# Experts' rows added to the stream in DRAM by scatters, instead of being gathered at the end

## The chip, the cores and the metric

The kernel runs on one core of a Trainium2 chip. The time is that of the device, in microseconds (us), the median of several executions. The core has a tensor engine (PE), three other compute engines (DVE, ACT, POOL), a queue processor that issues DMAs (SP), and 16 DMA engines that all queues share.

## The reference

One layer of a hybrid decoder for 512 tokens of 1024 values, all in float32. What matters here is its last part, the experts:

```python
h  = h + concat(rmsnorm_A(oA), rmsnorm_B(oB)) @ w_out      # attention, two groups of heads
h  = h + cross-attention(rmsnorm(h) -> rmsnorm(mem))
h  = h + hierarchical MoE(rmsnorm(h))   # top-1 group of 4, then top-2 of its 4 SwiGLU experts
out = rmsnorm_final(h)
```

There are 16 experts in 4 groups. Each has a gate and an up matrix (1024 x 256) and a down matrix (256 x 1024): 3.15 MB of weights. A token goes to two experts of one group, and their results come back to it with a weight each.

## The kernel before

The first three quarters of the span are the projections, the attentions and the router. The residual stream of the 512 tokens is held in SBUF as `HO`, four tiles (t = 0 to 3) of 128 tokens by 1024 values. The router writes the normed tokens to a DRAM tensor `T`, and for each expert a list of its tokens (up to 128 places, `lists`; with more, a path that this input doesn't take).

Then 16 experts follow one another (e = 0 to 15). For each:

- SP loads the weights in six units of 512 KB (four of gate and up, in two DMAs of 256 KB each, and two of down, one DMA each; line L736) into a ring of buffers, far ahead.
- POOL gathers the expert's rows of `T` into `xe` with an indirect DMA (L1130), four experts ahead.
- ACT casts each unit into a high part `wh` (L708) and DVE makes the low part `wl` (L709); PE multiplies with three products of parts for one product (L136 to L138).
- PE's sums for gate and up go through a sigmoid on ACT (`sg`, L1216) and DVE, are transposed, and ACT casts them into `hh` (L1229). Then PE does the down projection (`dn`).
- ACT scales the result by the tokens' weights into `y` (128 places by 1024, L1263; three buffers), and SP writes `y` to the expert's rows of a DRAM tensor `Y` (L1264). A row of zeros stands at the end of `Y`.

This holds for experts 0 to 13. The last two (`LATE = NE - 2`) don't go through DRAM: their rows stay in SBUF in two parts (L1252, L1253), DVE makes one-hot matrices `P` of their tokens' places (L1213), and PE spreads their rows over the tokens by products with `P` (`combine`, L1193), 32 matmuls in all. While expert 14 runs, POOL begins eight indirect gathers with accumulation `HO<-Y,slot` (L1269): for each tile of tokens and each of a token's two choices they fetch the row of `Y` with the number in `slot` and add it to `HO` in SBUF. A choice that is a late expert fetches the zero row. The two gathers of one tile must follow one another.

At the end POOL loads the gain of the last norm (L1279), DVE adds PE's sums to `HO` (L1288), ACT sums the squares (L1289), DVE multiplies by the norm and the gain (L1296), and SP writes the output (L1298).

The order of the instructions on each engine is set by a scheduler from the order of the code and from the tiles' buffers; an engine, and a DMA queue, takes its instructions in that order.

Of the kernel before, what the change touches and what calls it, by code (L numbers as in the profile page):

```python
# [11 lines left out]
F32 = mybir.dt.float32  # L12
# [9 lines left out]
S = 512  # L22
D = 1024
# [11 lines left out]
LATE = NE - 2  # L35
# [3 lines left out]
def layer(ctx, tc, a, out, dbg=None):  # L39
# [24 lines left out]
    # ---------------------------------------------------------------- helpers  # L64
    # a weight unit is 1024 values a partition: loaded whole, then split into two float32r parts
    W = {}

    # the places of a weight's tiles, in turn: (pool, tag count) for the raw unit and for its parts
# [71 lines left out]
    # -------------------------------------------------------------- constants  # L140
# [17 lines left out]
    # ================================================= phase 1: projection, FoX, SB  # L158
# [43 lines left out]
    # ---- forget gates  # L202
# [20 lines left out]
    # ---- pieces  # L223
# [82 lines left out]
    # what the heads give, by feature: the heads of a pair share a tile  # L306
# [3 lines left out]
    # the tokens come last first: the keys of a query block are its own block and those behind it;  # L310
    # the products of a pair's heads run side by side in the columns of the tensor engine
# [15 lines left out]
    # blocks of queries that are handled together  # L327
# [16 lines left out]
    # the features of a pair of heads go to their place; their squares are summed over the pairs  # L344
# [141 lines left out]
    # ================================================= memory keys and values  # L486
# [45 lines left out]
    # ================================================= phase 2: out projection, cross attention  # L532
# [16 lines left out]
    # the products of each run of a weight's rows are finished on their own  # L549
# [95 lines left out]
    # two heads of two tiles of tokens  # L645
# [47 lines left out]
    # ================================================= router  # L693
# [5 lines left out]
    # half a unit split: the parts take turns in halves of tiles  # L699
# [42 lines left out]
    Y = dram.tile([LATE * CAP + 1, D], F32, name="Y")  # L742
    # the token and the weight of every place in the experts' lists; rows of their own for what has none
    L = dram.tile([NE * CAP + 2 * S, 2], I32, name="L")
    zero8 = rt.tile([128, 8], F32, name="zero8")
    nc.gpsimd.memset(zero8, 0.0)
    nc.gpsimd.dma_start(Y[LATE * CAP:, :].rearrange("o (p c) -> (o p) c", p=128), zero8)
    zeroi = rt.tile([128, NE, 2], I32, name="zeroi")
    nc.gpsimd.memset(zeroi, 0)
    nc.gpsimd.dma_start(L[0:NE * CAP, :].rearrange("(p e) c -> p e c", e=NE), zeroi)  # L750
    # the gain of the norm goes into the router's weights, so that the router reads HO itself
# [30 lines left out]
    # of two equal logits the first wins: (i, 0, j) is one for j < i, (i, 1, j) for j > i  # L782
# [10 lines left out]
    # what a place holds, by token and choice: the token, then the bits of the weight  # L793
    put = rp.tile([128, 2, NT, 2], I32, name="put")
    nowhere = rtile([2, NT], "nowhere")
    for n in range(2):
        nc.gpsimd.iota(put[:, n, :, 0], pattern=[[128, NT]], base=0, channel_multiplier=1)
# [22 lines left out]
    # one half of a token tile of HO through the router's product  # L820
# [20 lines left out]
    def route(t):  # L841
# [8 lines left out]
        # the rank of a logit among the four of its set: the groups, or the experts of a group  # L850
# [14 lines left out]
        # places of the tile's tokens in the lists of their experts, plus one  # L865
# [9 lines left out]
        # the first expert's tokens come from HO itself: a one-hot of their places times the norm  # L875
# [41 lines left out]
    # the last experts' rows are spread by the tensor engine: their tokens (plus one) by place  # L917
    lidx = rp.tile([128, NE - LATE], F32, name="lidx")
    lists = rp.tile([128, NE, 2], I32, name="held")
    idx = rp.tile([128, FIRST], I32, name="idx")  # L920
    cnti = rp.tile([128, NE + 1], I32, name="cnti")
    slots, places = [], []
# [31 lines left out]
    # the place of a token's choice in the list of its expert, and its expert  # L954
# [35 lines left out]
    def slot_numbers(step):  # L990
        for n, (pv, ev, ok) in [(step, places[step])] if step < 2 else ():
            in_y = rtile([NT], f"iny{n}")
            nc.vector.scalar_tensor_tensor(in_y, ev, float(LATE), ok, op0=OP.is_lt, op1=OP.mult)
            sf = rtile([NT], f"sf{n}")
            nc.vector.scalar_tensor_tensor(sf, ev, float(CAP), pv, op0=OP.mult, op1=OP.add)
            nc.vector.scalar_tensor_tensor(sf, sf, float(-LATE * CAP), in_y, op0=OP.add, op1=OP.mult)
            nc.vector.tensor_scalar(sf, sf, float(LATE * CAP), None, op0=OP.add)
            si = rp.tile([128, NT], I32, name=f"slot{n}")
            nc.vector.tensor_copy(si, sf)
            slots.append(si)  # L1000
        if step < 2:
            return
        cmax = rp.tile([128, 1], F32, name="cmax")
        nc.vector.reduce_max(cmax, cnt, axis=AX.X)
        nc.vector.tensor_copy(cnti[:, 0:NE], cnt)
        nc.vector.tensor_copy(cnti[:, NE:NE + 1], cmax)
# [15 lines left out]
    # ================================================= experts with more than CAP tokens  # L1022
# [101 lines left out]
    # ================================================= experts  # L1124
# [65 lines left out]
    # the rows of a late expert, spread over a tile of tokens  # L1190
# [5 lines left out]
    for e in range(NE):  # L1196
# [9 lines left out]
        if e in (4, 6, 8):  # L1206
            with tc.issue_after(W["hid"].ins):
                slot_numbers(e // 2 - 2)
# [10 lines left out]
        if e == NE - 1:  # L1219
            spread = [dnp.tile([128, 512], F32, name="dn") for _ in range(2)]  # L1220
            for nh in range(2):
                combine(spread[nh], 0, nh, 0)
# [33 lines left out]
        # the weights of the first experts come late  # L1256
        if not late:
            waiting.append((e, y, dps))
        if e not in range(1):
            for n, y, dps in waiting:  # L1260
                with tc.issue_after(W["last"].ins):
                    for nh in range(2):
                        nc.scalar.activation(y[:, nh * 512:nh * 512 + 512], dps[nh], AF.Copy, scale=wof(n))  # L1263
                nc.sync.dma_start(Y[n * CAP:(n + 1) * CAP, :], y)  # L1264
            waiting.clear()
        if e == LATE:
            for n in range(2):
                for t in range(NT):
                    nc.gpsimd.indirect_dma_start(  # L1269
                        out=HO[:, t, :], out_offset=None, in_=Y[:, :],  # L1270
                        in_offset=bass.IndirectOffsetOnAxis(ap=slots[n][:, t:t + 1], axis=0),
                        compute_op=OP.add)
# [3 lines left out]
    # ================================================= combine, final norm  # L1276
    mark("combine")
    g_fin = etile([D])
    nc.gpsimd.dma_start(g_fin, a["norm_final"].partition_broadcast(128))  # L1279
    junk = etile([2, 512], F32)  # L1280
    for t in range(NT):
        ss = small.tile([128, 2], F32, name="ssf")
        for nh in range(2):
            cs = slice(nh * 512, nh * 512 + 512)
            cp = spread[nh] if t == 0 else dnp.tile([128, 512], F32, name="dn")
            for n in range(1 if t == 0 else 0, NE - LATE):
                combine(cp, t, nh, n)
# [39 lines left out]
```

## Time and profile before

| | us |
|---|---|
| median of 3 runs (664.9 to 665.46) | 665.44 |
| span of the profiled execution | 662.1 |
| PE busy in it | 625.6 (94%) |
| DVE, ACT, POOL busy | 461.6, 376.7, 53.1 |
| share of the chain that ended last: PE, DMA | 82%, 6% |

The profiled execution has no time of its own beside its span; the three runs' times are 665.46, 665.44 and 664.9 us. The span goes from the first to the last instruction of the core. A DMA isn't an instruction of an engine that computes: its issue is short, and its landing comes later. The DMA share is the mean busy share of the 16 DMA engines; the fullest windows of this profile show a little over 1.

### The profile page before, as it was taken

To read this page: it belongs to the slowest core of one execution; us is meant where nothing else is said; L and a number is where in the kernel's file an instruction comes from. 1 tells how busy PE (TensorE), PEld (TensorE's weight loads), DVE (VectorE), ACT (ScalarE), POOL (GpSimd) and SP (SyncE) were. 2 spreads that over 40 slices of the span, in tenths; PEclk is the share of its full clock that TensorE was granted. 3 is DMA by queue.
4 is the path that set the end of the run, shared out by engine and by line. 5 is a ranking of instruction groups with operands and counts; after the bars stand their busy time and mean duration, and the time that the engine had idled before them with its cause. 6 is when DMAs were issued, how large, how long until landed. Compare 5 with 4: busy or idle time off the path is not lost.

```text
span 662.1 us, 10336 instructions
## 1 busy us (share of the span) xinstructions
PE 625.6 (94%) x3595; PEld 507.4 (77%) x3596; DVE 461.6 (70%) x941; ACT 376.7 (57%) x752; POOL 53.1 (8%) x80
## 2 busy tenths in 40 slices
PE   3999999999999999999999999999999999999980
PEld 2988777888877888988888898867767777777750
DVE  4843794963497797855853466347879999989955
ACT  5632556653456676613632354333369898898842
POOL 2000000000000000000000003000152011010350
PEclk9999999999999999999999999999999999999996
DMA  8545744323764634561453223792989999999494
GB/s 279 171 125 133 186 113 116 92 65 92 171 157 107 169 104 152 200 218 35 121 166 96 77 84 88 260 367 99 313 258 366 378 388 380 386 383 385 130 201 174
DMA packets 105497, 128.91 MB, mean 195 GB/s; under 512 B 8456, under 2 KB 82240, under 8 KB 105440
## 3 DMA queue, kind: packets, MB, share of 16 engines
q1 hardware_dynamic: 101120, 114.43, 54.8%
q0 software_dynamic: 4320, 13.77, 7.6%
q8 instruction: 29, 0.48, 0.3%
q14 instruction: 28, 0.23, 0.1%
HBM read 103.96 MB, written 11.56 MB: 174 GB/s over the span
## 4 chain that ended last, share of the span: by engine, by line
PE 82%; DMA 6%; DVE 4%; ACT 3%; issue 2%; POOL 1%; SPq 1%; DVEq 0%; POOLq 0%
PE pj L136 8%; PE pj L138 8%; PE pj L137 8%; PE o L315 5%; PE gu L136 4%; PE pja L136 4%; PE gu L137 4%; PE gu L138 4%; PE pja L137 4%; PE pja L138 4%; PE tr L322 3%; PE tr L129 3%; PE pjb L137 3%; PE pjb L136 3%; PE pjb L138 3%; PE dn L136 2%
## 5 line engine op out<-in xcount | busy, mean ns | idle before, releaser
L90 DVE TENSOR_TENSOR wl<-w,wh 128x1024 fp32r<-128x1024 f32 (+1 forms) x64 | 78.3, 1223 | 81.3 <-ACT wh L89 75.1
L89 ACT CAST wh<-w 128x1024 fp32r<-128x1024 f32 (+1 forms) x64 | 67.2, 1050 | 104.5 <-PE pj L137 37.3
L709 DVE TENSOR_TENSOR wl<-w,wh 128x512 fp32r<-128x512 f32 x168 | 108.5, 686 | 5.5 <-ACT wh L708 5.1
L708 ACT CAST wh<-w 128x512 fp32r<-128x512 f32 x168 | 96.6, 621 | 12.8 <-PE gu L138 9.8
L136 PE MATMUL pj<-uh,wh 128*128 128x512 f32 x128 | 52.1, 407 | 0.0
L138 PE MATMUL pj<-uh,wl 128*128 128x512 f32 x128 | 51.5, 403 | 0.0
L137 PE MATMUL pj<-ul,wh 128*128 128x512 f32 x128 | 51.2, 400 | 0.0
L136 PE MATMUL gu<-wh,xh 128*128 128x512 f32 x120 | 48.5, 404 | 0.2 <-ACT xh L131 0.2
L138 PE MATMUL gu<-wh,xl 128*128 128x512 f32 x120 | 47.6, 397 | 0.0
L137 PE MATMUL gu<-wl,xh 128*128 128x512 f32 x120 | 47.1, 393 | 0.0
L136 PE MATMUL pj<-wh,uh 128*128 128x256 f32 (+1 forms) x128 | 37.7, 294 | 2.3 <-ACT uh L131 2.3
L138 PE MATMUL pj<-wh,ul 128*128 128x256 f32 (+1 forms) x128 | 37.5, 293 | 0.0
L137 PE MATMUL pj<-wl,uh 128*128 128x256 f32 (+1 forms) x128 | 37.3, 292 | 0.0
L315 PE MATMUL o<-pT,V 128*64 128x128 f32 x320 | 33.0, 284 | 0.1
L136 PE MATMUL pja<-wh,fmh 128*128 128x512 f32 x80 | 32.4, 405 | 0.0
L137 PE MATMUL pja<-wl,fmh 128*128 128x512 f32 x80 | 31.9, 399 | 0.0
L138 PE MATMUL pja<-wh,fml 128*128 128x512 f32 x80 | 31.8, 398 | 0.0
L315 PEld LDWEIGHTS o<-pT,V 128*64 128x64 f32 x320 | 21.4, 136 | 10.0 <-issue 5.2
L136 PEld LDWEIGHTS pj<-uh,wh 128*128 128x128 f32 x128 | 24.1, 188 | 6.3 <-issue 1.7
L138 PEld LDWEIGHTS pj<-uh,wl 128*128 128x128 f32 x128 | 24.1, 188 | 5.9 <-issue 0.9
L368 ACT ACTIVATE p<-lg,nm 128x512 f32<-128x512 f32 (+3 forms) x32 | 16.9, 527 | 20.4 <-DVE nm L366 20.3
L137 PEld LDWEIGHTS pj<-ul,wh 128*128 128x128 f32 x128 | 24.1, 188 | 4.8 <-issue 0.3
(356 smaller groups left out, 1633.2 us busy)
## 6 DMA issues: line engine op xcount, KB each, us to landing
w<-in_w_exp_gate_dram SPq DMA_DIRECT2D x64, 256.0 KB, 7.6
w<-in_w_exp_up_dram SPq DMA_DIRECT2D x64, 256.0 KB, 7.6
w<-in_w_exp_down_dram SPq DMA_DIRECT2D x32, 512.0 KB, 7.6
w<-in_w_in_dram SPq DMA_DIRECT2D x24, 512.0 KB, 4.1
w<-in_w_xkv_dram SPq DMA_DIRECT2D x16, 512.0 KB, 4.4
Y<-y SPq DMA_DIRECT2D x14, 512.0 KB, 8.7
KH<-th SPq DMA_DIRECT2D x32, 128.0 KB, 2.3
w<-in_w_out_dram SPq DMA_DIRECT2D x8, 512.0 KB, 4.3
```

Of the source, the lines that this page charges most:

```text
L89: nc.scalar.copy(h, raw)
L90: nc.vector.tensor_sub(l, raw, h)
L129: nc.tensor.transpose(pt[:, j, :], src[:, k * 128:(k + 1) * 128], ident)
L136: nc.tensor.matmul(o, lh, rh, start=start, stop=False)
L137: nc.tensor.matmul(o, lh, rl, start=False, stop=False)
L138: nc.tensor.matmul(o, ll, rh, start=False, stop=stop)
L315: nc.tensor.matmul(o[hh * HD:(hh + 1) * HD, i * 128:(i + 1) * 128], V[:, s, vcol + hh * HD:vcol + (hh + 1) * HD], pTs[hh][:, at + s - i, : ...
L322: nc.tensor.transpose(pt[:, s, :], p[:, s * 128:(s + 1) * 128], ident)
L368: nc.scalar.activation(p_[:, cs], lg[:, cs], AF.Exp, bias=nm, scale=1.0, accum_out=sm)
L708: nc.scalar.copy(h, raw)
L709: nc.vector.tensor_sub(l, raw, h)
```

## The change

A DRAM tensor `H2` (512 rows and 128 spare ones) gets the stream `HO` when the router has read it, by four writes on SP's queue. `y` of experts 0 to 14 is not written to a place of its own but added to its tokens' rows of `H2`, by an indirect DMA with accumulation on POOL's queue (a scatter, one for each expert); the lists get a third column with the row to add to, and empty places add to the spare rows. When the last scatter has landed, SP loads the four tiles of `HO` back from `H2`, and the gain of the last norm too. Only expert 15 is spread by one-hot products (`LATE = NE - 1`): 16 matmuls, none of them ahead of its own down projection. `Y`, its zero row, the numbers `slot` and the eight gathers are gone.

```diff
-LATE = NE - 2
+LATE = NE - 1
...
-    Y = dram.tile([LATE * CAP + 1, D], F32, name="Y")
+    H2 = dram.tile([S + CAP, D], F32, name="H2")
-    L = dram.tile([NE * CAP + 2 * S, 2], I32, name="L")
+    L = dram.tile([NE * CAP + 2 * S, 3], I32, name="L")
...
         nc.sync.dma_start(T[t * 128:(t + 1) * 128, :], u)
+        nc.sync.dma_start(H2[t * 128:(t + 1) * 128, :], HO[:, t, :])
...
-        if e in (4, 6, 8):
+        if e == 8:
             with tc.issue_after(W["hid"].ins):
-                slot_numbers(e // 2 - 2)
+                counts()
...
-        if e == NE - 1:
-            spread = [dnp.tile([128, 512], F32, name="dn") for _ in range(2)]
-            for nh in range(2):
-                combine(spread[nh], 0, nh, 0)
...
-                nc.sync.dma_start(Y[n * CAP:(n + 1) * CAP, :], y)
+                nc.gpsimd.indirect_dma_start(
+                    out=H2[:, :], out_offset=bass.IndirectOffsetOnAxis(ap=lists[:, n, 2:3], axis=0),
+                    in_=y, in_offset=None, compute_op=OP.add)
             waiting.clear()
         if e == LATE:
-            for n in range(2):
-                for t in range(NT):
-                    nc.gpsimd.indirect_dma_start(
-                        out=HO[:, t, :], out_offset=None, in_=Y[:, :],
-                        in_offset=bass.IndirectOffsetOnAxis(ap=slots[n][:, t:t + 1], axis=0),
-                        compute_op=OP.add)
+            g_fin = etile([D])
+            nc.sync.dma_start(g_fin, a["norm_final"].partition_broadcast(128))
+            for t in range(NT):
+                nc.sync.dma_start(HO[:, t, :], H2[t * 128:(t + 1) * 128, :])
...
-    g_fin = etile([D])
-    nc.gpsimd.dma_start(g_fin, a["norm_final"].partition_broadcast(128))
```

POOL's instructions in the experts' stage, before: the gathers of the experts' rows stand one behind another, and behind them the eight accumulating gathers of the end and the gain.

```order
L1130 DMA xe<-T,idx 128x1024
L1130 DMA xe<-T,held 128x1024 x12
L1269 DMA HO<-Y,slot_5675 128x1024 x4
L1269 DMA HO<-Y,slot_5905 128x1024 x4
L1279 DMA w<-in_norm_final_dram 128x1024
L1029 TENSOR_LOAD cnti
```

POOL's instructions now, in the middle of the stage (`y_5802`, `y_5913` and `y_6024` are the rows of experts 5, 6 and 7, `xe_5852` is expert 9's, and each scatter also waits for the scatter before it to land):

```order
L1120 DMA xe_5852<-T_4375,held_5085 128x1024
L1250 DMA H2_4376<-y_5802,held_5085 640x1024
L1120 DMA xe_5963<-T_4375,held_5085 128x1024
L1250 DMA H2_4376<-y_5913,held_5085 640x1024
L1250 DMA H2_4376<-y_6024,held_5085 640x1024
L1120 DMA xe_6074<-T_4375,held_5085 128x1024
L1120 DMA xe_6189<-T_4375,held_5085 128x1024
L1250 DMA H2_4376<-y_6139,held_5085 640x1024
```

Between the gathers now stand the scatters, one for each expert to 14, so that a gather can have a scatter ahead of it that waits; the gathers of the end are gone.

SP's end of the stage, before: the last weight loads (the two of the down matrix are expert 15's), then the writes of experts 12 and 13, then the output.

```order
L736 DMA w<-in_w_exp_gate_dram 128x2x256
L736 DMA w<-in_w_exp_up_dram 128x2x256
L736 DMA w<-in_w_exp_down_dram 128x1024 x2
L1029 TENSOR_LOAD cnti
L1029 ISA x2
L1264 DMA Y<-y 128x1024 x2
L1298 DMA out_dram<-w 128x512 x8
```

The same end of SP's queue now:

```order
L736 DMA w_6720<-in_w_exp_down_dram 128x1024
L736 DMA w_6722<-in_w_exp_down_dram 128x1024
L1019 TENSOR_LOAD cnti_5087
L1019 ISA x2
L1258 DMA HO_81<-H2_4376 128x1024 x3
L1256 DMA w_6899<-in_norm_final_dram 128x1024
L1258 DMA HO_81<-H2_4376 128x1024
L1282 DMA out_0_dram<-w_6929 128x512 x2
```

The writes of `y` have left SP's queue, where they stood behind the weights, and the four loads of `HO` and the gain stand ahead of the output.

ACT's instructions while expert 14 ends, now (they stand the same way before, with `w_6732` and L1229; `w_6720` is the first down unit of expert 15, `hh_6789` and `y_6801` are expert 14's):

```order
L708 CAST wh_5259<-w_6711 128x512
L1206 ACTIVATE sg_6783<-gu_6742 128x256
L708 CAST wh_5259<-w_6714 128x512
L708 CAST wh_5261<-w_6720 128x512
L1215 CAST hh_6789<-tr_6786 128x256
L708 CAST wh_5262<-w_6720 128x512
L708 CAST wh_5260<-w_6714 128x512
L1249 ACTIVATE y_6801<-dn_6802,held_5085 128x512
```

Nothing moved here: in both kernels a cast of expert 15's down unit stands ahead of expert 14's `hh`.

## Rows read from the trace of the kernel before

**Rows 1.** The page: the span
```profile
span 662.1 us, 10336 instructions
```

**Rows 2.** Timeline of DVE at the end: start, length (us), line, operation
```profile
650.93 0.68 DVE L1288 TENSOR_TENSOR HO<-dn,HO 128x512 f32<-128x512 f32 x1
...
655.07 1.41 DVE L1296 SCALAR_TENSOR_TENSOR w<-HO,rr,w 128x512 f32<-128x512 f32 x2
```

**Rows 3.** Windows: busy us (count) by engine, granted clock, DMA share, GB/s
```profile
475.00:495.00 20.00, 18.45 (x81) 11.55 (x78) 16.36 (x61) 10.29 (x19) 11.50 (x11) 1.00 0.86 276
495.00:500.00 5.00, 4.97 (x24) 3.60 (x23) 4.50 (x10) 4.85 (x11) 0.97 (x1) 1.00 0.76 238
500.00:520.00 20.00, 19.95 (x93) 15.21 (x92) 18.33 (x38) 18.08 (x36) 2.42 (x2) 1.00 1.06 379
612.00:614.00 2.00, 2.00 (x10) 1.50 (x8) 1.43 (x4) 1.91 (x5) 0.00 (x0) 1.00 1.00 401
614.00:616.00 2.00, 1.97 (x13) 1.55 (x12) 2.00 (x5) 1.46 (x4) 0.00 (x0) 1.00 0.40 147
624.00:628.00 4.00, 4.00 (x18) 2.88 (x18) 4.00 (x9) 2.92 (x6) 3.39 (x3) 1.00 0.72 114
628.00:646.00 18.00, 15.52 (x61) 10.61 (x60) 10.16 (x24) 8.03 (x18) 9.47 (x7) 1.00 1.05 202
```

**Rows 4.** Timeline of ACT, experts 0, 13 and 14
```profile
496.73 1.27 ACT L1263 ACTIVATE y<-dn,held 128x512 f32<-128x512 f32 x2
...
614.50 0.37 ACT L1229 CAST hh<-tr 128x256 fp32r<-128x256 f32 x1
...
623.26 1.13 ACT L708 CAST wh<-w 128x512 fp32r<-128x512 f32 x2
624.36 0.38 ACT L1229 CAST hh<-tr 128x256 fp32r<-128x256 f32 x1
...
628.04 0.69 ACT L1252 ACTIVATE w<-dn,held 128x512 fp32r<-128x512 f32 x1
```

**Rows 5.** Waits of SP's DMA queue: total us, times, longest
```profile
SPq L736 <- DMA w<-in_w_exp_gate_dram: 17.7, 32, 1.9
SPq L736 <- DMA w<-in_w_exp_up_dram: 14.4, 26, 1.8
SPq L736 <- DMA w<-in_w_exp_down_dram: 14.1, 15, 1.9
```

**Rows 6.** Timeline of SP's issues near the end
```profile
607.07 1.04 SPq L736 DMA_DIRECT2D w<-in_w_exp_down_dram  x2
609.37 10.19 SPq L1264 DMA_DIRECT2D Y<-y  x2
```

**Rows 7.** Line L736, the one load issued between 607.5 and 608 us
```profile
L736 SPq DMA_DIRECT2D w<-in_w_exp_down_dram x1: 340/340/340, 607.8 to 607.8; - x1
...
DMA to landing us min/median/max: 8.3/8.3/8.3
```

**Rows 8.** The chain that ended last, its end
```profile
629.08 9.07 DMA HO<-Y,slot
...
639.84 9.53 DMA w<-in_norm_final_dram
```

**Rows 9.** Line L1269, the first accumulating gather (issued 622.7)
```profile
DMA to landing us min/median/max: 6.7/6.7/6.7
```

**Rows 10.** Line L736, a lone weight load, 512 KB (issued 461.9)
```profile
DMA to landing us min/median/max: 3.1/3.1/3.1
```

**Rows 11.** Waits of the engines, 500 to 618 us
```profile
POOL xe L1130 <- PE tr L129: 89.9, 11, 9.2
```

**Rows 12.** DMA issues: count, KB each, median us to landing
```profile
Y<-y SPq DMA_DIRECT2D x14, 512.0 KB, 8.7
...
xe<-T,held POOLq DMA_INDIRECT x12, 7.5
...
HO<-Y,slot POOLq DMA_INDIRECT x8, 9.1
```

More of the change, by code (lines that the diff above doesn't have):

```diff
@@ L741, in layer @@
     T = dram.tile([S, D], F32, name="T")
-    Y = dram.tile([LATE * CAP + 1, D], F32, name="Y")
-    L = dram.tile([NE * CAP + 2 * S, 2], I32, name="L")
[L745 to L750, printed above, removed]
+    H2 = dram.tile([S + CAP, D], F32, name="H2")
+    L = dram.tile([NE * CAP + 2 * S, 3], I32, name="L")
+    none = rt.tile([128, NE, 3], I32, name="none")
+    nc.gpsimd.memset(none, 0)
+    nc.gpsimd.iota(none[:, :, 2], pattern=[[0, NE]], base=S, channel_multiplier=1)
+    nc.gpsimd.dma_start(L[0:NE * CAP, :].rearrange("(p e) c -> p e c", e=NE), none)
     grow = nw.tile([KT, 128], F32, name="gain", bufs=1)
@@ L792, in layer @@
                    allow_small_or_imprecise_dtypes=True)
-    put = rp.tile([128, 2, NT, 2], I32, name="put")
+    put = rp.tile([128, 2, NT, 3], I32, name="put")
     nowhere = rtile([2, NT], "nowhere")
     for n in range(2):
-        nc.gpsimd.iota(put[:, n, :, 0], pattern=[[128, NT]], base=0, channel_multiplier=1)
+        for c in (0, 2):
+            nc.gpsimd.iota(put[:, n, :, c], pattern=[[128, NT]], base=0, channel_multiplier=1)
     nc.gpsimd.iota(nowhere, pattern=[[S, 2], [128, NT]], base=NE * CAP, channel_multiplier=1,
@@ L918, in layer @@
     lidx = rp.tile([128, NE - LATE], F32, name="lidx")
-    lists = rp.tile([128, NE, 2], I32, name="held")
+    lists = rp.tile([128, NE, 3], I32, name="held")
     idx = rp.tile([128, FIRST], I32, name="idx")
     cnti = rp.tile([128, NE + 1], I32, name="cnti")
-    slots, places = [], []
+    places = []
     w1 = rp.tile([128, NT], F32, name="w1")
@@ L988, in late_tokens, with counts @@
         nc.vector.tensor_scalar(lidx, lidx, 1.0, None, op0=OP.add)
[L990 to L1002, printed above, removed]
+    def counts():
         cmax = rp.tile([128, 1], F32, name="cmax")
@@ L1284, in layer @@
             cs = slice(nh * 512, nh * 512 + 512)
-            cp = spread[nh] if t == 0 else dnp.tile([128, 512], F32, name="dn")
-            for n in range(1 if t == 0 else 0, NE - LATE):
+            cp = dnp.tile([128, 512], F32, name="dn")
+            for n in range(NE - LATE):
                 combine(cp, t, nh, n)
```

## The prediction

> **What bounds the kernel now.** I read the page first, for the span and the engines' shares. The profiled span is 662.1 us [rows 1], and by the page PE is busy for nearly all of it. The median of the three runs is 665.44 us, so 3.3 us lie around the span. Everything below is worked out on the clock of the trace. The last multiplication on DVE ends at 655.07 + 1.41 = 656.5 us [rows 2], and I take it that the median moves with this point: 665.4 - 656.5 = 8.9 us always stand behind it.
>
> The second view is the table of windows, for the experts' stage [rows 3]. From 500 to 520 us (and with nearly the same numbers in each of the four windows to 600, and up to 612) PE is busy for 19.95 of 20 us, and at the same time the 16 DMA engines are full: a share of 1.06 at 379 to 386 GB/s. So this stage has two limits side by side. PE needs 9.86 us for an expert, which is the distance of the casts of `hh` of two experts, 614.50 and 624.36 us [rows 4]. In that time an expert's weights (3.15 MB), its gathered rows (0.52 MB) and its written rows (0.52 MB) are 4.19 MB, and 4.19 MB at 383 GB/s are 10.9 us. The weights live on a lead that was built earlier, and it is eaten up by about 1.1 us for each expert. The waits of SP's queue say the same: the weight loads wait for earlier weight loads to land, 46 us in all [rows 5].
>
> How much of the lead is left at the end? The last two weight loads, expert 15's down weights, are issued together at 607.07 us [rows 6], the second at 607.8. The second lands 8.3 us after its issue [rows 7], at 616.1. The one ahead of it is 0.524 MB, or 1.37 us at 383 GB/s, earlier: 614.7 us. The windows agree, the rate falls from 401 to 147 GB/s between 612 and 616 us [rows 3]. The first of these units is cast by ACT as the second of the pair at 623.26 us, so at about 623.8 [rows 4]. **The lead is 623.8 - 614.7 = 9.1 us.** ACT has expert 14's hidden values (`hh`) right behind that cast, and so expert 14's down projection and its rows, which are ready at 628.04 + 0.69 = 628.7 us.
>
> The third view is the chain that ended last, for the tail [rows 8]: the gathers of the written rows with accumulation hold POOL's queue until the gain of the last norm can be issued at 639.84 us. Its 9.53 us end at 649.4, and only then do the last multiplications start.
>
> **The change, part by part.**
> *The tail with nothing late.* Expert 14's scatter goes out behind `y` at about 628.9 us. An accumulating gather that met little other traffic took 6.7 us to land [rows 9]; with that the scatter is there at 635.6. Then SP loads HO's four parts and the gain, 0.52 MB each. A lone load of this size landed after 3.1 us [rows 10], so the first is there at 638.8, and the fifth 4 × 1.37 us later, at 644.2. The additions of the last token tile end about 1.4 us later, at 645.6. Before, the last addition ended at 650.93 + 0.68 = 651.6 and the last multiplication 4.9 us after it [rows 2]. Now all eight multiplications of 0.72 us and the small steps stand behind the last load, so some 7 us: 652.6 us. Against 656.5 that is **a gain of 3.9 us.**
>
> *The DMA's work in the stage.* Fourteen plain writes of 0.524 MB, 1.37 us of all DMA engines each at 383 GB/s, become fifteen scatters that also read what they add to. The trace has no scatter, but it has accumulating gathers with rows of the same length. Between 628 and 646 us nearly nothing else is on the DMA engines, and they are full (1.05) at 202 GB/s [rows 3]: 0.524 / 0.202 = 2.60 us for one. That is the low bound. The start of the same gathers, 624 to 628 us, moved 114 GB/s × 4 us = 0.456 MB with 0.72 × 4 = 2.88 us of share: 2.88 / 1.05 × 0.524 / 0.456 = 3.15 us for one, the high bound. A scatter has its accumulated side in DRAM, not in SBUF; I see no row that prices this. I take the steady row, 2.60, as the nearest: 1.23 us more than a plain write.
>
> The Trainium skill bears on this ("Collectives: The Full Stack", section "The bandwidth ceiling: the fold count and why AG ≠ RS ≠ AR"): the add costs no cycles of its own but needs two source reads, and its measured ratio is 1.93, so a scatter would be estimated at 1.93 × 1.37 = 2.64 us, and the whole time by it at about 673 us. The trace agrees, 383 / 202 GB/s is 1.9. This rule speaks against the change.
>
> *When the weights then land.* Ahead of expert 15's first down unit lie the scatters of experts 0 to 11, with their extra of 1.23 us each, 14.8 us. The writes of experts 12 and 13 stood behind the weights on SP's queue (the two at 609.37 [rows 6]), so they cost the weights nothing. Now they go through POOL's queue and share the engines with the weights as soon as these are late, so each counts whole, 2 × 2.60 = 5.2 us. Together 20.0 us: the unit lands at 634.7 instead of 614.7 us, **10.9 us after ACT wants it**. The lateness shows from about expert 13 on, as waits of ACT's `wh` and so of PE. Expert 14's `hh`, its rows, its scatter and the tail move by the same 10.9 us: 652.6 + 10.9 = 663.5, 7.0 us behind 656.5. **665.4 + 7.0 = 672.5 us.** With 3.15 us for a scatter it is 12 × 1.78 + 6.3 = 27.7 us, 18.6 late, 680.1 us. With 2.60 and only expert 12's scatter counted whole it is 17.4 us, 8.3 late, 669.8 us.
>
> *What costs nothing.* The four writes of HO to H2 (2.1 MB, 5.5 us) come before 500 us, where the windows leave (1.06 - 0.86) × 20 + (1.06 - 0.76) × 5 = 5.5 us of DMA unused [rows 3]. T's last write has the same bytes ahead of it as before. I take 0; without that cover the lead shrinks by up to 5.5 us, which is within the high bound. On POOL, the gathers of experts 11 and later now stand behind scatters that wait; they are wanted some three experts (30 us) later, and POOL waits 89.9 us there for PE and is otherwise idle [rows 11]. The slot numbers on DVE, four of the eight one-hot products, half of the combining matmuls and SP's issue of the writes fall away beside work that goes on anyway: 0, since PE and DVE wait for DMA in the tail.
>
> **The rivals.**
> *The lead hides it.* The scatters might take few engine-microseconds (the added-to rows lie in the same DRAM, and a gather from DRAM that counts bytes once is not a scatter). The delay is 9.1 us or less if 12 (x - 1.37) + 2x ≤ 9.1, so x ≤ 1.82 us for a scatter. Then the tail's gain stands alone: 665.4 - 3.9 = 661.5 us. For it: no scatter has been seen. Against it: 1.82 is well below both rows.
>
> *The gain and the delay cancel.* Between x = 1.82 and 2.1 us the weights are 0 to 3.9 us late: 664 to 667 us.
>
> *The chain of scatters sets the end.* Every scatter waits for the one before it to land, from 498.0 us on, when the rows of expert 0 are there (496.73 + 1.27 [rows 4]), and a `y` tile is written anew only when the scatter three back has landed. Beside the weights a plain gather lands after 7.5 us and a plain write after 8.7; the queued accumulating gathers took 9.1 [rows 12]. In the forecast expert 14's scatter lands at 628.9 + 10.9 + 6.7 = 646.5. With the last two scatters at 6.7 us, thirteen loaded ones reach that when each takes (646.5 - 13.4 - 498.0) / 13 = 10.4 us. That is the point from which the chain decides, and it is not far above 9.1. At 11 us the chain ends at 654.4, 7.9 later: 680 us; at 11.5 us 687 us. Against it: an extra 1.2 us on a plain gather's 7.5 is 8.7.
>
> The Trainium skill would never let this chain bind ("DMA: Bandwidth & Descriptors", section "Anatomy of one DMA — SWDGE (gpsimd) path"): its fit for a DMA from this queue, 2.0 us plus the bytes at 436 GB/s, is 3.2 us for a scatter. The trace disagrees, with 7.5 us for the loaded gathers of this size [rows 12].
>
> **How the numbers follow.** Forecast (DMA-bound, 668 to 681): 0.47. Chain of scatters (675 to 690): 0.25. Hidden by the lead (about 661.5): 0.17. Cancelled (664 to 667): 0.08. The rest, 0.03, is beyond. A measurement here tells 0.2%, 1.3 us, from no change. So faster 0.17, same 0.08, slower 0.75. The range, 661 to 687 us, takes in the hidden case and leaves out the slow end of the chain and little else. The forecast's own range is 668 to 681.
>
> **What would show it.** Right: in the windows of 520 to 600 us DMA stays full but moves fewer GB/s; from expert 12 or 13 on PE loses busy time, ACT's `wh` waits for DMA loads of weights, and expert 15's first down unit lands near 635 us; the time from the last scatter's landing to the last multiplication is about 17 us. The chain of scatters would show as POOL waiting in every expert for `H2<-y` and scatters of over 10 us. The forecast is wrong if PE stays at 9.86 us an expert to the end, or if the DMA share of the stage leaves room.

## The result, and the profile after

The changed kernel takes 670.8 us (median of 4 runs, 669.3 to 671.33) beside 665.17 us of the kernel before on the same chip: a ratio of 1.0088, 95% interval [1.0071, 1.0106], 5.6 us slower. The forecast was 672.5 us. Its direction and its size came true, but the wait that the trace of the changed kernel shows is not the one that the forecast put first.

The page of the changed kernel, its span and the queue of POOL's DMAs (packets, megabytes, share of 16 engines' span):

```profile
span 669.5 us, 10294 instructions
...
q0 software_dynamic: 5152, 16.92, 9.9%
```

The windows of the changed kernel answer to [rows 3]:

```profile
485.00:490.00 5.00, 4.76 (x17) 3.43 (x16) 2.60 (x5) 2.29 (x5) 3.85 (x4) 0.66 1.10 367
500.00:520.00 20.00, 19.95 (x93) 15.32 (x92) 18.31 (x35) 18.23 (x36) 6.85 (x4) 1.00 1.07 338
540.00:560.00 20.00, 19.95 (x93) 15.31 (x92) 18.19 (x33) 18.02 (x35) 6.04 (x4) 1.00 1.07 336
560.00:580.00 20.00, 17.17 (x80) 13.16 (x78) 16.96 (x34) 16.86 (x33) 6.58 (x4) 1.00 1.07 338
580.00:600.00 20.00, 17.75 (x76) 13.86 (x77) 14.35 (x26) 14.21 (x28) 5.78 (x4) 0.91 1.07 340
628.00:630.00 2.00, 2.00 (x10) 1.66 (x9) 1.85 (x4) 2.00 (x5) 0.00 (x0) 1.00 0.64 143
```

The DMA engines are as full as before (1.06 to 1.07), but move 336 to 340 GB/s where it was 379 to 386. They stay full (1.03 to 1.09) beyond 614 us, until about 628 us. PE is busy without a gap to 560 us, then loses 2.8 us, and 2.2 more by 600 us. So PE's loss comes in the middle of the stage, not near its end, where the forecast had it. The timeline of ACT (answering to [rows 4]) puts it between two experts; these are the casts of `hh` of experts 9, 10 and 14, and the second half of expert 14's `y`:

```profile
577.21 0.37 ACT L1215 CAST hh<-tr 128x256 fp32r<-128x256 f32 x1
...
593.36 0.37 ACT L1215 CAST hh<-tr 128x256 fp32r<-128x256 f32 x1
...
632.76 0.37 ACT L1215 CAST hh<-tr 128x256 fp32r<-128x256 f32 x1
...
636.44 0.69 ACT L1249 ACTIVATE y<-dn,held 128x512 f32<-128x512 f32 x1
```

Before, the last of these three casts was at 624.36 us [rows 4], and the first two here:

```profile
575.04 0.37 ACT L1229 CAST hh<-tr 128x256 fp32r<-128x256 f32 x1
...
584.90 0.37 ACT L1229 CAST hh<-tr 128x256 fp32r<-128x256 f32 x1
```

Expert 9 is 2.2 us late, expert 10 is 8.5 us late, and it stays so: expert 14's rows are ready at 637.1 instead of 628.7 us. Of the waits of the engines between 500 and 640 us, one is new on PE:

```profile
PE tr L129 <- DMA xe<-T,held: 5.1, 1, 5.1
```

PE waits for gathered rows. POOL's timeline shows which, and why they are late (the scatters of experts 5, 6 and 7 are the rows of 551.05, 560.92 and 571.49, expert 10's gather that of 553.45, expert 11's that of 573.84):

```profile
551.05 2.09 POOL L1250 DMA_INDIRECT H<-y,held  x1 [7.17 <-ACT wh L708]
553.45 1.28 POOL L1120 DMA_INDIRECT xe<-T,held  x1 [0.30 <-PE gu L137]
560.92 2.07 POOL L1250 DMA_INDIRECT H<-y,held  x1 [6.19 <-ACT wh L708]
571.49 2.05 POOL L1250 DMA_INDIRECT H<-y,held  x1 [8.50 <-ACT wh L708]
573.84 1.01 POOL L1120 DMA_INDIRECT xe<-T,held  x1 [0.30 <-PE gu L138]
```

In the kernel before, POOL's timeline has expert 11's gather here, and PE's timeline the first use of its rows:

```profile
560.17 1.08 POOL L1130 DMA_INDIRECT xe<-T,held  x1 [8.65 <-PE tr L129]
```

```profile
574.84 0.60 PE L129 MATMUL tr<-ident,xe 128*128 128x128 f32 x4
```

Expert 11's gather stands behind expert 7's scatter on POOL's queue, expert 7's scatter waits for expert 6's to land, and so the gather goes out 13.7 us later. (The row of 571.49 names a cast of ACT as what ended the wait. Expert 7's rows were there 9 us earlier, at 562.5 us, so what is left is the scatter before it, whose landing this trace doesn't show; in two_chains below, where a scatter doesn't wait for the one before it, expert 7's goes out at 559.43 us, when its rows are there.) The gather lands at 573.84 + 8.22 = 582.1 us; PE wants these rows at 577 us and stands still for 5.1 us.

The distance of the two casts grew by more than that, by 6.3 us. The other 1.2 us go with PE's granted clock, the last number but two of these rows: PE takes up its work at half speed, the lower of its two levels (1.2 and 2.4 GHz).

```profile
582.00:584.00 2.00, 1.77 (x7) 1.61 (x8) 0.03 (x1) 0.59 (x1) 0.80 (x1) 0.50 1.05 385
584.00:586.00 2.00, 2.00 (x8) 1.63 (x7) 1.86 (x3) 0.63 (x2) 0.00 (x0) 0.73 1.09 372
```

The chain that ended last has that step, and at its end the loads of the stream (compare [rows 8]):

```profile
573.84 8.22 DMA xe<-T,held
...
646.81 7.75 DMA HO<-H
```

SP's queue (compare [rows 6]) has the last weight loads at 621 us instead of 607, and the first load of `HO` at 645.0 us; and the last addition and multiplications on DVE (compare [rows 2]) are these:

```profile
621.21 1.08 SPq L736 DMA_DIRECT2D w<-in_w_exp_down_dram  x2
645.01 1.28 SPq L1258 DMA_DIRECT2D HO<-H  x3
```

```profile
655.46 0.68 DVE L1272 TENSOR_TENSOR HO<-dn,HO 128x512 f32<-128x512 f32 x1
...
659.82 2.74 DVE L1280 SCALAR_TENSOR_TENSOR w<-HO,rr,w 128x512 f32<-128x512 f32 x4
```

The last multiplication ends at 659.82 + 2.74 = 662.6 us, 6.1 us later than before. The parts: 2.2 us before expert 1, 6.3 us for expert 11's gather (5.1 of standing, 1.2 of lower clock), together 8.4 us with rounding; 1.8 us because expert 14's scatter, with its rows ready at 637.1, waits until 638.9 for expert 13's to land; and about 4 us that the new tail is shorter, as forecast.

### The profile page after: what moved, and what is told of

Read it like the earlier page. It is cut to its first block, busy times and chain, and to the rows that moved or that the text cites. A ratio compares the mean times of both kernels' runs of the same rounds, so it can differ in the third digit from the quotient of the medians.

```text
span 669.5 us, 10294 instructions
## 1 busy us (share of the span) xinstructions
PE 624.5 (93%) x3579; PEld 506.7 (76%) x3580; DVE 458.7 (69%) x925; ACT 376.2 (56%) x752; POOL 65.9 (10%) x87
## 3 DMA queue, kind: packets, MB, share of 16 engines
q0 software_dynamic: 5152, 16.92, 9.9%
## 4 chain that ended last, share of the span: by engine, by line
PE 83%; DMA 6%; DVE 5%; ACT 3%; issue 2%; SPq 1%; ACTq 0%; DVEq 0%
PE pj L136 8%; PE pj L137 8%; PE pj L138 8%; PE o L315 4%; PE gu L136 4%; PE gu L138 4%; PE gu L137 4%; PE pja L136 4%; PE pja L137 4%; PE pja L138 4%; PE tr L322 3%; PE tr L129 3%; PE pjb L137 3%; PE pjb L136 3%; PE pjb L138 3%; PE dn L136 2%
## 5 line engine op out<-in xcount | busy, mean ns | idle before, releaser
L708 ACT CAST wh<-w 128x512 fp32r<-128x512 f32 x168 | 96.4, 621 | 14.7 <-PE gu L138 10.9
L1250 POOL DMA_INDIRECT H<-y,held x15 | 26.2, 1750 | 86.0 <-ACT wh L708 61.7
```

The source lines that it names most:

```text
L708: nc.scalar.copy(h, raw)
L1250: nc.gpsimd.indirect_dma_start(out=H2[:, :], out_offset=bass.IndirectOffsetOnAxis(ap=lists[:, n, 2:3], axis=0), in_=y, in_offset=None, com ...
```

## The experiments

Three theories stood against each other. The **weights theory** is the forecast: the scatters' additional work on full DMA engines makes the weights late. The **chain theory**: each scatter waits for the one before it, and these links set the time. The **order theory**: only the gather's place on POOL's queue costs time. Each kernel was timed beside the kernel before, and the ratios are to that one. Its median was not the same each time (665.17 us beside the change; 663.31 beside gathers_first, two_chains, no_add and h2_later; 664.92 beside gathers_first_two_chains and the first three skip_empty runs; 663.67 beside the others), so rows of different groups are compared by their ratios. Each trace is of one execution.

| kernel | us | ratio [95% interval] |
|---|---|---|
| the change | 670.8 | 1.0088 [1.0071, 1.0106] |
| gathers_first | 670.66 | 1.0115 [1.0086, 1.0144] |
| two_chains | 671.07 | 1.0097 [1.0059, 1.0136] |
| gathers_first_two_chains | 669.83 | 1.0081 [1.0058, 1.0105] |
| no_add | 658.98 | 0.9927 [0.9899, 0.9955] |
| h2_later | 671.64 | 1.0132 [1.0089, 1.0174] |
| four_weights_reused | 665.76 | 1.0031 [1.0013, 1.005] |
| skip_empty | 666.6 | 1.0045 [1.0023, 1.0068] |
| skip_empty_gathers_first | 668.07 | 1.0052 [1.003, 1.0074] |
| skip_empty_14_scattered | 664.54 | 0.9996 [0.9977, 1.0016] |
| skip_empty_spread | 667.16 | 1.0046 [1.0029, 1.0063] |
| skip_both_spread | 665.65 | 1.0027 [1.0014, 1.0041] |
| before_plain_gathers | 665.69 | 1.0034 [1.0021, 1.0048] |

### Taking the stall away: gathers_first, two_chains, and both

The first edit lets each scatter be issued only behind the gather of the expert four further on:

```diff
-                nc.gpsimd.indirect_dma_start(out=H2[:, :], ...)
+                ready.append((n, y))
...
         xn = head(e + 1) if e + 1 < NE else None
+        scatter()      # what is ready, within tc.issue_after(W["xe"].ins)
```

> On POOL's queue each expert's gather now stands ahead of the scatter that it stood behind (the scatter of expert k behind the gather of expert k+4); nothing else is changed. The order theory: the changed kernel loses its time only where PE waits for expert 11's gathered rows, which stood behind the scatters of experts 6 and 7; that stall (6.3 us on the distance of hh of experts 9 and 10) goes and the time falls from 670.8 to about 664.5. The chain theory: each scatter waits for the one before it, one link is 9.9 us, and the chain from expert 0's scatter at 500.5 to expert 14's at 638.9 us is never short of rows; it ends at the same time, so the time stays at 670 to 672 though PE's stall is gone. The weights theory (the forecast): without the stall expert 15's down weights come about 5 us too late, ACT's wh waits for them, about 669 to 670.

The second gives the scatters of odd experts a tensor of their own:

```diff
-                    out=H2[:, :], out_offset=...
+                    out=(H3 if n % 2 else H2)[:, :], out_offset=...
```

> The scatters of odd experts go to a second tensor of the same size, so that a scatter waits for the one two before it. Left out: the second tensor is neither filled with zeros nor added back, so that the bytes moved are the same. The chain theory: no scatter waits any more, expert 11's gather comes in time, expert 14's rows are ready at about 631 us and its scatter goes at once: 670.8 - 6.3 - 1.7, about 662.8. The weights theory: the scatters move as many bytes and the same additions, so without the stalls expert 15's down weights are about 5 us late: 667 to 668, with ACT's wh waiting for DMA.

The third has both:

> Both edits together: each gather ahead of the scatter it stood behind, and the scatters of odd experts on a second tensor. Left out: the second tensor is neither filled with zeros nor added back; bytes and additions are the same. Neither the order nor the chain can cost anything here. The weights theory: the DMA engines' work is unchanged, so expert 15's (and before it expert 13's and 14's) down weights come late and ACT's wh waits for them some 6 us; the time stays at 670 to 672. The chain theory and the order theory: 661 to 663.

Each of the three takes 670 to 671 us, and their ratios lie around that of the change: no gain that can be measured. PE's wait for expert 11's rows is gone in all three, and a wait for weights stands in its place. Waits between 500 and 640 us, of gathers_first, two_chains and both, one fence each:

```profile
ACT wh L708 <- DMA w<-in_w_exp_down_dram: 2.8, 1, 2.8
```

```profile
ACT wh L708 <- DMA w<-in_w_exp_down_dram: 6.5, 2, 3.9
```

```profile
ACT wh L708 <- DMA w<-in_w_exp_down_dram: 4.7, 2, 3.6
```

In the kernel with both edits, where neither place nor chain can hold anything up, the timeline of ACT shows the casts of `hh` of experts 11 to 14 and the longest of the waits, in brackets at the end of its row:

```profile
596.94 0.37 ACT L1227 CAST hh<-tr 128x256 fp32r<-128x256 f32 x1
...
607.98 0.37 ACT L1227 CAST hh<-tr 128x256 fp32r<-128x256 f32 x1
...
620.92 0.62 ACT L708 CAST wh<-w 128x512 fp32r<-128x512 f32 x1 [3.56 <-DMA w<-in_w_exp_down_dram]
621.44 0.37 ACT L1227 CAST hh<-tr 128x256 fp32r<-128x256 f32 x1
...
632.87 0.37 ACT L1227 CAST hh<-tr 128x256 fp32r<-128x256 f32 x1
```

The distances are 11.0, 13.5 and 11.4 us instead of 9.86: 6.4 us are lost in experts 12 to 14. The waits for down weights are 4.7 of them. Most of the rest is the granted clock again, right behind the longest wait; at 0.57 for 4 us it costs some 1.7 us:

```profile
622.00:626.00 4.00, 4.00 (x11) 3.13 (x12) 3.04 (x7) 1.67 (x4) 0.00 (x0) 0.57 1.10 369
```

This is the forecast's mechanism, with a lower clock on top that the forecast didn't have, and in sum nearly the size of the stall that it replaces (6.3 us). In the changed kernel the DMA engines stayed full (1.05) from 577 to 582 us while PE stood, and no cast of ACT waited for weights there. The chain theory and the order theory fall as causes of the whole: the order theory expected 664.5 us of the first kernel, the chain theory 662.8 of the second, and both 661 to 663 of the third. The weights theory missed too, by 3 us in the second kernel (667 to 668 expected): there the distances from expert 10 to 14 grow by 11 us, 6.5 of them waits for weights and most of the rest lower clock (0.50 between 622 and 626 us). In the first kernel expert 14's scatter still waits 2.6 us for the one before it.

### Taking the DMA's work away: no_add and four_weights_reused

```diff
-                    in_=y, in_offset=None, compute_op=OP.add)
+                    in_=y, in_offset=None)
```

> The scatters write instead of adding; left out is the addition, the order and the waits between the scatters are the same. If the addition costs 1.2 us of the DMA engines, as the rates of before say, the windows from 520 to 560 us go back from 338 to about 380 GB/s. The chain theory: a link falls from 9.9 to about 8.5 us, below PE's 9.86 us an expert, so the lag doesn't build up, the stall goes and expert 14's scatter waits for nothing: about 662 to 663.5. The weights theory gives the same time, 662 to 663.5, by the lead that is kept. The order theory (the place on POOL's queue alone costs the time, whatever a scatter takes): 669 to 671.

It takes 658.98 us, 4.3 us less than the kernel before beside it (663.31). That is a larger gain than expected (662 to 663.5 beside 665.17, so 1.7 to 3.2 us). Its window answers to that of 540 us above:

```profile
540.00:560.00 20.00, 19.95 (x93) 15.11 (x91) 18.19 (x36) 18.00 (x36) 5.07 (x4) 1.00 1.06 384
```

The rate is back at 384 GB/s. From the two rates the price of the addition follows. In 9.86 us the changed kernel moves 9.86 × 0.340 = 3.35 MB (0.340 from its windows of 520 and 540 us, 344 and 336), of which 0.524 MB are a scatter. The other 2.83 MB take 7.34 us at 385 GB/s, which leaves 2.52 us for the scatter with its addition, against 1.36 us without: 1.2 us for the addition. POOL's queue on the page says nearly the same with the same packets and bytes, 9.9% of the 16 engines' span of 669.5 us against 7.0% of 658.6:

```profile
q0 software_dynamic: 5152, 16.92, 7.0%
```

That is 66.3 against 46.1 us, so 1.35 us for each of the 15 additions.

But two things went with the addition. The links of the chain are shorter too: the first five scatters, which still wait for one another, are 8.6 us apart on the mean (499.42 to 533.92 us), less than PE's 9.86 us, so that the chain catches up with the rows. And the last scatter lands sooner, 4.0 us from issue to the first load of `HO` (630.10 and 634.06 us), instead of 6.1, which neither theory had counted:

```profile
630.10 0.96 POOL L1250 DMA_INDIRECT H<-y,held  x1 [8.54 <-DVE wl L709]
```

```profile
634.06 1.28 SPq L1258 DMA_DIRECT2D HO<-H  x3
```

The other way to make room is fewer weights:

```diff
-            raws[n] = pre[n] if n < NPRE else eunit(n)
+            raws[n] = pre[n] if n < NPRE else raws[n - 6] if e in (7, 9, 11, 13) else eunit(n)
```

> The changed kernel, but experts 7, 9, 11 and 13 compute with the weights of the expert before them, which aren't loaded again (left out: their own weights, 12.6 MB); casts, products, gathers and scatters are the same in number. The weights theory in its full form: a scatter's additional work costs time only because the DMA engines are full. With this room the weights come in time, the links of the chain get shorter, expert 11's gather comes in time: 661 to 663.5. If a link of the chain of scatters is about 10 us whatever else the DMA engines do, expert 11's gather stays late and so does the last scatter: 668 to 671.

665.76 us, between the two ranges. The windows and the one wait for gathered rows:

```profile
560.00:580.00 20.00, 16.64 (x77) 12.71 (x76) 16.41 (x31) 16.31 (x32) 7.78 (x5) 1.00 0.93 273
...
600.00:610.00 10.00, 9.97 (x47) 7.66 (x46) 9.53 (x20) 8.97 (x18) 3.25 (x2) 1.00 0.53 108
```

```profile
PE tr L129 <- DMA xe<-T,held: 3.7, 1, 3.7
```

The room came only after 560 us, when expert 11's gather was already held up: it goes out at 573.31 us (573.84 in the changed kernel) and PE still waits for it. Behind it no weight is late, with the DMA share at 0.53, and expert 14's scatter goes out as soon as its rows are there (635.79 us). So this run doesn't separate the theories as it was meant to; it shows that the stall on POOL's queue is there whatever happens to the weights afterwards.

### The writes of the stream: h2_later

```diff
-        nc.sync.dma_start(H2[t * 128:(t + 1) * 128, :], HO[:, t, :])     # in route(), beside T
...
+    with tc.issue_after(W["T"].ins):
+        for t in range(NT):
+            nc.sync.dma_start(H2[t * 128:(t + 1) * 128, :], HO[:, t, :])
```

> The four writes of the stream to H2 stand behind the last write of T on SP's queue instead of between the writes of T. If their place costs the 2.2 us by which expert 1's hh is later than in the kernel before, expert 1's hh and with it the first scatter come up to 2.2 us earlier, and all behind them: 668.6 to 669. If the 2.2 us come from the bytes themselves (2.1 MB before 500 us) or from the wider lists, no change, 670 to 671.5.

Nothing came back: the casts of `hh` of experts 0 and 1 are 11.54 us apart, as in the changed kernel, and 10.41 us in the kernel before. But in no_add and two_chains, which have the same writes, they are 10.41 us apart too. What goes with the 1.1 us is PE's granted clock: 0.66 between 485 and 490 us in the change, in gathers_first and in h2_later, 1.00 in the kernel before, in no_add and in two_chains. (In skip_empty_gathers_first and skip_empty_14_scattered the distance is 11.6 and 12.6 us at a clock of 1.00; there PE stands between 494 and 498 us, another loss.) Why the clock fell in some kernels and not in others is not shown. The other 1.1 us stand at expert 0 already, and that point lies between 484.9 and 487.6 us over these runs; they are not shown to come from the change.

### Fewer rows: the runs that leave out empty places

A list has 128 places, and half of them are empty on the mean. Their row number lies past the stream's 512 rows, so one argument leaves them out:

```diff
-                    in_=y, in_offset=None, compute_op=OP.add)
+                    in_=y, in_offset=None, bounds_check=S - 1, oob_is_err=False, compute_op=OP.add)
```

> The changed kernel, but the scatter's empty places (a list has 128 places; 512 tokens with two experts each fill 64 of them on the mean over 16 experts) have a row number past the bound, and the DMA leaves such rows out. Order and waits are the same. The weights theory: a scatter's work on the DMA engines falls from 2.5 to about 1.25 us, less than a plain write of all places (1.37 us), so the weights keep their lead: 659 to 661 us. The chain theory: a link falls well below 9.86 us: the same. The order theory (place on POOL's queue alone): 668 to 671.

> Skipping the empty places, and each gather ahead of the scatter it stood behind. If scatters of half the rows no longer hold POOL's queue up, the second edit adds nothing: 659 to 661 us, the same as with the first alone. If expert 11's gather still comes late there, 1 to 3 us less than with the first alone.

> Skipping the empty places, the gathers first, and two experts spread by one-hot products again as in the kernel before, so that the last scatter is expert 13's and the stream is loaded back while expert 15 is computed. If the loads of the stream after the last scatter are what is left of the wait at the end, 1 to 3 us less than with 15 scattered experts: 656 to 659. If DVE's additions and multiplications are already what ends last, no change: 659 to 661.

The second adds the edit of gathers_first, the third also `LATE = NE - 2`. The first two are 5.6 and 7.1 us above the highest time expected of them, the third 3.5 us. The page and a window of skip_empty:

```profile
q0 software_dynamic: 5152, 13.01, 7.3%
```

```profile
540.00:560.00 20.00, 19.95 (x93) 15.27 (x92) 18.18 (x35) 18.00 (x35) 6.88 (x5) 1.00 0.99 327
```

The bytes fell as planned (16.92 to 13.01 MB), the packets didn't (5152 in both), and the scatters still go out 9.6 us apart from expert 0's to expert 10's, little less than the 10.2 us of the change over the same ten links. The DMA engines now show a share of 0.99 and move 327 GB/s, where with all rows they showed 1.07 and moved 336. A share of 0.99 is less than full here: full windows show 1.06 or 1.07, and the four windows from 520 to 600 us of skip_empty show 0.95 to 1.01. The engines' work did fall: the queue's 7.3% of 663.8 us are 48.5 us, nearly the 46.1 of no_add. In both runs with 15 experts scattered no cast waits for weights between 500 and 640 us. So the weights theory's condition was met, and the time it promised didn't come.

What is left is the chain. With the gathers first, the second half of expert 14's `y` and its scatter stand here:

```profile
628.93 0.69 ACT L1260 ACTIVATE y<-dn,held 128x512 f32<-128x512 f32 x1
```

```profile
635.56 1.55 POOL L1192 DMA_INDIRECT H<-y,held  x1 [5.44 <-DVE hl L1228]
```

The rows are ready at 629.6 us, as early as in no_add (629.8), but the scatter goes out 5.9 us later, behind expert 13's, which went out at 628.26 us. So the chain alone can cost what the stall or the late weights cost.

Two more runs tried to explain the rate. The first permutes the places (`at = 16 (8 p - 127 (p div 16)) + e` for place p, and the same permutation in the one-hot products of experts 0 to 3); the second also leaves the empty places out of the gathers:

> Skipping the empty places gave 4 us, not 10, and left the DMA share at 0.95 to 1.0 at 305 to 330 GB/s. A theory for that: the filled places are the first ones of a list, and the rows of neighbouring places lie on the same DMA engines, so that half of the engines do all of a scatter's work, and each weight load waits for the slowest of them. Here the places of a list are spread over the partitions (place p at partition 8 (p mod 16) + p div 16). If that theory holds, the DMA rate of 520 to 600 us rises above 340 GB/s and the time falls to 660 to 663. If the rows lie on the engines in another way, it stays at 666 to 668.

> As skip_empty_spread, and the gathers of experts 4 to 15 leave the empty places out too. If the DMA engines' work is what costs the time, another 0.26 MB less for each expert keeps more of the weights' lead: 659 to 662. If skip_empty_spread's own theory fails, 662 to 667.

The theory of neighbouring rows falls: 313 to 326 GB/s with the places spread, and 667.16 us. With the gathers cut too it is 665.65 us, above the 659 to 662 expected, at 288 to 311 GB/s and a DMA share of only 0.89 to 0.96 from 520 to 600 us: the engines have room there, and the time doesn't fall.

### The kernel before, without accumulation

```diff
-                        out=HO[:, t, :], out_offset=None, in_=Y[:, :],
-                        in_offset=bass.IndirectOffsetOnAxis(ap=slots[n][:, t:t + 1], axis=0),
-                        compute_op=OP.add)
+                        out=got[t, n], out_offset=None, in_=Y[:, :],
+                        in_offset=bass.IndirectOffsetOnAxis(ap=slots[n][:, t:t + 1], axis=0))
...
+        for n in range(2):
+            nc.vector.tensor_add(HO[:, t, :], HO[:, t, :], got[t, n])
```

> The kernel before, with the eight gathers of its end into tiles of their own without accumulation, tile by tile of tokens, the additions on DVE (eight of 128 x 1024), and the gain of the last norm loaded early on SP's queue. If the accumulation on the DMA engines (2.6 us for a gather instead of 1.4) is what holds the end of that kernel, the last gather lands some 4 us earlier and the time falls by 3 to 6 us: 659 to 662. If POOL's issue of the gathers (1.6 to 2.0 us each) or DVE's additional work sets the end, no change, 663 to 666.

The gathers became cheap: POOL issues all eight by 632.6 us, where the kernel before was at 640.4. But the output isn't finished sooner. POOL's first and last gather, and SP's writes of the output:

```profile
622.27 0.94 POOL L1273 DMA_INDIRECT w<-Y,slot  x1 [22.48 <-ACT wh L708]
...
631.70 0.94 POOL L1273 DMA_INDIRECT w<-Y,slot  x1 [0.30 <-issue]
```

```profile
646.67 11.62 SPq L1301 DMA_DIRECT2D out_dram<-w  x8
```

The first write starts 3.6 us sooner (650.25 before), but the eight now spread over 11.6 us (6.6 before): DVE's additional additions (1.2 us each) stand between its multiplications. 665.69 us is 0.3% more than the kernel before.

## Why the prediction came out right, point by point

- **The DMA's work of a scatter**: 2.60 us forecast, 2.52 us by the two rates, 1.85 times the 1.36 us of a plain one. Right. Without the addition the change gains 4.3 us, near the 3.9 forecast for a tail with nothing late; that is in part chance, since a plain scatter also lands 2.1 us sooner, which the 3.9 don't contain. The Trainium skill's ratio of 1.93 for an add with its two source reads, taken there from collectives ("Collectives: The Full Stack", section "The bandwidth ceiling: the fold count and why AG ≠ RS ≠ AR") agrees with that within a twentieth.
- **The weights late**: the mechanism is right, but hidden in the changed kernel itself, where another stall stood in front of it. It shows as soon as that is removed. Its size was 10.9 us in the forecast and is 6.4 us in the run with both edits, of which 4.7 are waits for weights and some 1.7 a lower clock, for which the forecast had no term. The term that was too large is the second of the two whole scatters: expert 13's goes out behind the last weight loads there (627.87 us, the loads at 624.22), so it isn't ahead of expert 15's down weights. Counting one only, the forecast's own lower bound, gave 8.3 us; the 1.9 us from there to 6.4 aren't traced. The signs given for it, a loss of PE time from expert 12 or 13 on and ACT's waits for weights, are missing in the change and present in that run.
- **The gathers on POOL's queue**, which the forecast costed at nothing since they were "wanted some three experts (30 us) later": this step failed. In the kernel before, expert 11's gather goes out at 560.17 and PE transposes its rows from 574.84 us on, 15 us later, half of which the landing needs (7.5 us [rows 12]). It was held up for 13.7 us, and PE waited 5.1 us and then ran at a lower clock: 6.3 us.
- **The chain of scatters**: the links are (638.92 - 500.47) / 14 = 9.9 us, between the 9.1 that was thought likely and the 10.4 at which it was to decide. It doesn't set the end, apart from 1.8 us, but it is what holds the gather up. The first link takes 10.7 us (500.47 to 511.12), while expert 1's rows are ready at about 503.5, 4.9 us after its `hh`; the chain starts 7.6 us behind its rows and, with links longer than PE's 9.86 us, can't catch up. A rival with a threshold of its own became the cause of another step's failure. The Trainium skill's fit for this queue ("DMA: Bandwidth & Descriptors", section "Anatomy of one DMA — SWDGE (gpsimd) path"), by which a scatter is an estimated 3.2 us, doesn't hold here: 6.1 us for the last scatter, with little beside it, and 9 to 11 us from one scatter to the next in the stage.
- **The tail**: 3.9 us forecast. From the last scatter's issue to the last multiplication 23.6 us, forecast 23.7. Its parts (landing, loads, additions, multiplications) were forecast at 6.7, 8.6, 1.4 and 7.0 us and measured 6.1, 9.5, 1.6 and 6.4. Right.
- **The writes to H2** at nothing: up to 2.2 us appear before expert 1; half of it goes with a clock that was granted lower, and h2_later shows that their place isn't the cause.
- **The rival in which gain and delay cancel**: by its own terms (0 to 3.9 us late) it stands for 661.5 to 665.4 us, not for 664 to 667. The forecast's 672.5 us is 672.4 by its printed terms. Neither changes the result.

The sum came out at 7.0 us against a measured 5.6 because one stall of 6.3 us took the place of another of 6.4 us. This is shown by the three runs that remove the first. That the two are of one size, and the forecast so near, is luck: the step that costs the time in the changed kernel is the one that was put at nothing. That the addition is what costs is shown by no_add. It costs in two ways, which no_add takes away together: by its work on full DMA engines (late weights, shown by the run with both edits) and by the time that each scatter keeps the next one waiting (the late gather of the change, and 5.9 us at the end of skip_empty_gathers_first).

What stays open: why the links of the chain hardly shorten when half of a scatter's rows are left out, though the DMA engines have room, and shorten by more than 1 us without the addition. No version that does the whole work was found clearly faster than the kernel before; the nearest, skip_empty_14_scattered, is level with it.

## What to carry to other kernels

Where the DMA engines are full, price a new transfer by its time on them, not by its bytes: an accumulating transfer cost 1.85 times a plain one of the same size here, and a lead of 9 us was spent after a dozen of them. Where such transfers must wait for one another, compare the time of one link with the time of a step of the kernel as well: 9.9 us against 9.86 was enough for the chain never to catch up. Put a transfer that waits behind the loads that feed the next stages, on a queue that takes its entries in order, and read each load's real slack from the trace (its issue to its first use) before calling its delay free. When one stall is removed and the time doesn't move, look for the wait that took its place: two limits of nearly the same size can stand behind one number. And count a stall of PE with what the lower clock behind it costs.

## What the runs showed of the hardware that was not expected

- The packets of rows that a bound leaves out are still there: 5152 on that queue with and without them, while the bytes fall from 16.92 to 13.01 MB and the queue's time on the 16 engines from 66.3 to 48.5 us.
- A scatter beside the weight loads took 9 to 11 us from its issue to the next one's, whether its rows were all moved or half of them; with little else on the DMA engines the last one took 6.1 us with the addition (6.2 with half of its rows, in skip_empty) and 4.0 us without.
- PE's clock was granted at 0.66 of full speed on the mean between 485 and 490 us in six of these kernels, right behind a stretch (480 to 485 us) in which PE was busy for 2.5 to 3.3 of 5 us, and the distance of two experts' `hh` was up to 1.1 us longer with it; in no_add, with 2.98 of 5 us in that stretch, it stayed at 1.00.
- Behind a long stall PE did not start again at full speed: 0.50 of it between 582 and 584 us in the change, after 5.1 us of standing, and 0.57 between 622 and 626 us in the run with both edits, after 3.6 us. That made a stall of 5.1 us cost 6.3, and one of 4.7 us in all cost 6.4.
